# An encoder layer on one core: constant products and a pinned root at the start, stores on another queue, attention's pool in three, the last sums elsewhere

## The chip, the cores and the metric

The kernel runs on one core of one Trainium2 chip. A core has a matrix engine (TensorE; PE in the profile, with its weight loads as PEld), a vector engine (VectorE, DVE), an activation engine (ScalarE, ACT), a general engine (GpSimd, POOL) and a queue that mostly issues transfers (SyncE, SP). ACT issues transfers too; they stand in the profile as ACTq. Sixteen DMA engines move the data. Each engine works through its own instructions in the order in which they were laid down. The metric is the time of one execution in device microseconds; less is better.

## The reference, cut to what matters

One layer of a bidirectional encoder in float32, on 2048 rows of 1024 columns: a combined projection of the normed input, from which a Hyena part (long convolutions by FFT, 512 channels) and an mLSTM part (4 heads, both directions) are made; their output projection; cross-attention into 256 rows of `mem`; a squared-ReLU MLP; a final norm.

```python
u = _rms_norm(h, norm_mix_g[l])
proj = u @ w_in[l]
hy = _short_conv_centred(proj[..., :HY_COLS], hy_conv_w[l], hy_conv_b[l])
...
y_hy = _group_rms_norm(_hyena(hy, spec, hy_skip[l]), hy_norm_g[l], HYENA_GROUPS)
...
y_ml = _group_rms_norm(y_ml, ml_norm_g[l], MLSTM_HEADS)
mixed = jnp.concatenate([y_hy.astype(h.dtype), y_ml.astype(h.dtype)], axis=-1)
h = h + mixed @ w_out[l]
h = h + _cross_attention(_rms_norm(h, norm_x_g[l]), _rms_norm(mem, norm_mem_g[l]),
                         xa_wq[l], xa_wk[l], xa_wv[l], xa_wo[l])
h = h + jnp.square(jax.nn.relu(_rms_norm(h, norm_ff_g[l]) @ ff_w1[l])) @ ff_w2[l]
...
return _rms_norm(h, final_norm_g)
```

## The kernel before

**Products.** A float32 product is made of three products of rounded halves (`mm3`, L355): high by high, high by low, low by high, each 128x128 by 128x512, summed in a bank of PSUM. `split` (L367) makes the halves: ACT rounds, DVE subtracts. Two tags of four banks each, `mm` and `hy`, hold results.

**The order.** The code is a set of generators that hand over to each other (`program`, L2056): the input projection (`sweep`, `natural`) is woven with the filters, then with Hyena; the projections of `mem` (`memproj`, L684) with the first five steps of mLSTM (`take(m, 5)`, L2079); then attention (L1416) with the rest of mLSTM, by `weave`, which gives each side a share of time; then the MLP (`ffn`, L1772). What comes out is given to a planner, which orders each engine's instructions by its own estimate of times. An instruction that is *pinned* (`keep_in_program_order`) keeps its place among the pinned ones; `behind` puts an instruction after the last product so far.

**The start (L548).** The projection begins before the norm is known: the raw input, times the gain, is split into `xh` and `xl`, and the factor 1/rms of each row is applied when a bank is emptied (L780, by `rowb`). Of each half (c = 0, 1) of the first 1024 rows come: `operand` (the split), `squares` (ACT squares, DVE sums into `ssum`), `columns` (four products that sum over partitions, then `inv_rms` with a root by Newton steps in `rsqrt`, L224, then `diagonal`, which makes the tile `dg`), `rows` (a product that spreads the factors over partitions, copied to `rowb`). These pieces hang on hooks `(group, k)`: group is the number of the bank being filled, k the block of 128 inputs. Groups 0 to 3 are c = 0, 4 to 7 are c = 1, so the fifth group needs a bank that `rowb` has released.

**`memproj`.** For each of four heads `keys` multiplies a projection of `mem` with the query weights and stores four tiles `o` into `gd`; `values` does the same with the output weights into `vw`. A tile is copied out of its bank by ACT (`staged`, L704, tag `st`, three buffers) and stored from ACT's own queue (L718, L730). The weights of `mem` (`wm`) come over SP's queue. `natural` (L854) stores the mLSTM values and the sigmoid gates from ACT's queue too (L886).

**Pools.** `i_sb` (L437) holds all tiles of the projection phase. Attention's pool `t` (L1354) lies in the space that it and Hyena's pool leave, with `acc`, four activations, two pairs of weight halves and four staging tiles `wn`; what is first written there waits for the readers of what lay there. In attention `mixed` loads rows of Hyena's and mLSTM's outputs (L1452), turns them with the identity (L1458) and splits them; the first products of half the depth (L1510) need Hyena's rows alone.

**The end.** The second matrix of the MLP is done with seven products per pair of blocks (a Strassen-like scheme): seven sums `acc[i, tp]`, filled for four blocks o of the depth (L1965), and combined for the last block (o = 3) by `add` (L1958) on DVE (V) or POOL (G). `turned` turns a combined tile back, with its squares (L1929) and the gain (L1930); `finish` (L1932) takes the root and scales (L1942 on DVE, L1944 on ACT) and stores to the output. The last product of all is i = 4, tp = 1, and its four results are added at L1994.

Of the kernel before, what the change touches and what calls it, by code (L numbers as in the profile page):

```python
# [133 lines left out]
class Prog:  # L134
# [89 lines left out]
    def rsqrt(self, pool, ms, name):  # L224
# [5 lines left out]
        nc.vector.tensor_scalar(yi, mi, -0.5, float(0x5F3759DF), ALU.mult, ALU.add)  # L230
        for _ in range(3):
            nc.vector.tensor_tensor(t, y, y, ALU.mult)
            nc.vector.scalar_tensor_tensor(t, t, -0.5, ms, ALU.mult, ALU.mult)
            nc.vector.scalar_tensor_tensor(y, t, 1.5, y, ALU.add, ALU.mult)
# [147 lines left out]
    def weights(self, pool, w, n, kc=4, bufs=2, nbufs=2, pin=False):  # L382
# [4 lines left out]
        if n > 512:  # L387
            for k0 in range(kt):
                for c0 in range(0, n, 512):
                    cs = slice(c0, c0 + 512)  # L390
                    nat = pool.tile([128, 512], F32, tag="wn", name="wn", bufs=nbufs)
# [3 lines left out]
        for k0 in range(0, kt, kc):  # L395
            nat = pool.tile([128, kc, n], F32, tag="wn", name="wn", bufs=nbufs)
# [31 lines left out]
    def inproj_open(self, es):  # L428
# [7 lines left out]
        self.d_gt = self.dram("gt", (L, 16))  # L436
        sb = self.isb = es.enter_context(tc.tile_pool(name="i_sb", bufs=1))  # L437
# [21 lines left out]
    def inv_rms(self, dst, src):  # L459
        nc, sb, n = self.nc, self.isb, dst.shape[1]  # L460
        ms = sb.tile([128, 4], F32, tag="ms", name="ms", bufs=2)[:, 0:n]
        nc.vector.tensor_scalar(ms, src, 1.0 / D, EPS, ALU.mult, ALU.add)
        nc.vector.tensor_copy(dst, self.rsqrt(sb, ms, "xr"))

    def square_sum(self, x, dst):
        junk = self.isb.tile([128, 512], F32, tag="st", name="junk", bufs=3)
# [26 lines left out]
    def diagonal(self, cols):  # L493
        dg = self.isb.tile([128, 512], F32, tag="rb", name="dg", bufs=2)[:, 0:128 * cols.shape[1]]
        for t in range(cols.shape[1]):
            self.nc.vector.tensor_scalar(dg[:, 128 * t:128 * t + 128], self.ident, cols[:, t:t + 1], None, ALU.mult)
# [27 lines left out]
    def x_chunks(self, hf):  # L524
# [3 lines left out]
        def room(n):  # L528
            if not 1 < n < deep:
                return None  # L530
            t = self.isb.tile([128, 1088], F32, tag=("P", "cv")[n % 2], name="xt", bufs=2)
# [16 lines left out]
    def x_first(self):  # L548
# [10 lines left out]

        wsrc = self.items[0][0].rearrange("(k p) c -> p k c", p=128)  # L560
# [3 lines left out]
        for j in range(4):  # L564
            t = sb.tile([128, 1088], F32, tag=("P", "cv")[j // 2], name="xt", bufs=2)
# [5 lines left out]
        def operand(xs, c, k):  # L571
# [3 lines left out]
            nc.vector.scalar_tensor_tensor(self.xl[to], xs[k], g, self.xh[to].bitcast(F32), ALU.mult, ALU.subtract)  # L575

        def squares(xs, c):
            for k in range(8):
                sq = sb.tile([128, 512], F32, tag="st", name="sq", bufs=3) if k else ssum[c]
                pin(nc.scalar.activation(sq, xs[k], AF.Square))  # L580
                if k:
                    nc.vector.tensor_tensor(ssum[c], ssum[c], sq, ALU.add)

        def columns(c):
# [8 lines left out]
            self.inv_rms(rx, p[:, 0:4])  # L593
            self.dg = self.diagonal(rx)
# [1554 lines left out]
```

## Time and profile before

| | us |
|---|---|
| median of 3 runs | 3109.32 (3107.85 to 3111.45) |
| the profiled execution | 3110.14 |
| its span, first to last instruction | 3108.4 |
| PE busy | 3025.3 |
| DVE busy | 1955.3 |
| ACT busy | 1497.7 |
| POOL busy | 1141.1 |

A row of a timeline gives the start in us, the duration, engine, line, operation, what is written and read with the shapes, and in brackets the idle time before it and what released it. A row of waits gives the total, the number and the longest. A row of stretches gives the stretch and its length, the busy time of PE, PEld, DVE, ACT and POOL with counts, the granted TensorE clock (1 is full), the share of DMA time used, and GB/s. The clock has no record for the first 12 us; there the distance between products shows it.

### The profile page before, as it was taken

To read this page: it belongs to the slowest core of one execution; us is meant where nothing else is said; L and a number is where in the kernel's file an instruction comes from. 1 tells how busy PE (TensorE), PEld (TensorE's weight loads), DVE (VectorE), ACT (ScalarE), POOL (GpSimd) and SP (SyncE) were. 2 spreads that over 40 slices of the span, in tenths; PEclk is the share of its full clock that TensorE was granted. 3 is DMA by queue.
4 is the path that set the end of the run, shared out by engine and by line. 5 is a ranking of instruction groups with operands and counts; after the bars stand their busy time and mean duration, and the time that the engine had idled before them with its cause. 6 is when DMAs were issued, how large, how long until landed. Compare 5 with 4: busy or idle time off the path is not lost.

```text
span 3108.4 us, 42926 instructions
## 1 busy us (share of the span) xinstructions
PE 3025.3 (97%) x14257; PEld 2374.5 (76%) x14257; DVE 1955.3 (63%) x3429; ACT 1497.7 (48%) x2931; POOL 1141.1 (37%) x802
## 2 busy tenths in 40 slices
PE   8999999999999998999999999999999999999998
PEld 6655667776676766888887888888888788888876
DVE  7865465446756456877664566657554676565696
ACT  6543466533656225565544455556555443333335
POOL 0122011200222333333132337766466375243693
PEclk9999999999999999999999999999999999999999
DMA  6654768576878996565476557657644565354435
GB/s 211 190 198 163 231 207 251 178 232 194 254 203 241 302 300 220 158 199 170 143 250 206 197 172 235 207 178 238 200 153 153 171 210 182 109 166 118 157 93 172
DMA packets 444102, 607.07 MB, mean 195 GB/s; under 512 B 38494, under 2 KB 248542, under 8 KB 442856
## 3 DMA queue, kind: packets, MB, share of 16 engines
q1 hardware_dynamic: 405988, 546.54, 55.2%
q10 hardware_dynamic: 37892, 57.79, 5.5%
q8 instruction: 113, 1.85, 0.2%
q14 instruction: 109, 0.89, 0.1%
HBM read 401.79 MB, written 202.41 MB: 194 GB/s over the span
## 4 chain that ended last, share of the span: by engine, by line
PE 55%; DVE 3%; DMA 1%; issue 1%; ACT 1%; POOL 0%; SPq 0%; DVEq 0%; POOLq 0%; ACTq 0%
PE mm L361 12%; PE mm L357 12%; PE mm L360 12%; PE hy L357 6%; PE hy L361 6%; PE hy L360 6%; DVE bl L1668 1%; PE hy L1310 1%; PE hy L1312 1%; DVE acc L1960 0%; PE hy L1458 0%; DVE acc L1994 0%; PE hy L1571 0%; DMA va<-vd 0%; PE hy L1272 0%
## 5 line engine op out<-in xcount | busy, mean ns | idle before, releaser
L1668 DVE TENSOR_TENSOR bl<-wr,bh 128x512 fp32r<-128x512 f32 x213 | 242.1, 1142 | 127.6 <-ACT bh L1667 122.9
L1667 ACT CAST ah<-w 128x512 fp32r<-128x512 f32 x284 | 176.5, 622 | 301.1 <-PE hy L360 155.9
L368 DVE TENSOR_TENSOR wl<-wn,wh 128x512 fp32r<-128x512 f32 (+1 forms) x296 | 213.1, 765 | 101.0 <-ACT wh L368 100.4
L357 PE MATMUL mm<-xh,wh 128*128 128x512 f32 x640 | 267.5, 419 | 8.5 <-ACT wh L368 7.9
L1024 POOL TENSOR_TENSOR b<-b,a 128x512 f32<-128x512 f32 x64 | 87.0, 1362 | 509.4 <-ACT b L1022 238.8
L360 PE MATMUL mm<-xl,wh 128*128 128x512 f32 x640 | 253.7, 397 | 1.3 <-DVE xl L368 1.3
L361 PE MATMUL mm<-xh,wl 128*128 128x512 f32 x640 | 254.8, 399 | 0.0
L1667 ACT CAST bh<-wr 128x512 fp32r<-128x512 f32 x232 | 143.5, 621 | 230.2 <-PE mm L361 172.6
L1668 DVE TENSOR_TENSOR al<-w,ah 128x512 fp32r<-128x512 f32 x236 | 216.0, 916 | 55.5 <-ACT ah L1667 54.1
L357 PE MATMUL mm<-bh,ah 128*128 128x512 f32 x576 | 225.2, 391 | 1.8 <-DVE acc L1830 1.7
L361 PE MATMUL mm<-bh,al 128*128 128x512 f32 x576 | 223.3, 390 | 2.6 <-POOL al L1668 2.6
L360 PE MATMUL mm<-bl,ah 128*128 128x512 f32 x576 | 224.4, 390 | 0.0
L368 ACT CAST wh<-wn 128x512 fp32r<-128x512 f32 (+1 forms) x296 | 164.2, 618 | 109.4 <-PE mm L361 52.7
L360 PE MATMUL mm<-act,wh 128*128 128x512 f32 x512 | 202.3, 395 | 0.0
L361 PE MATMUL mm<-act,wl 128*128 128x512 f32 x512 | 200.5, 393 | 0.9 <-DVE wl L368 0.9
L357 PE MATMUL mm<-act,wh 128*128 128x512 f32 x512 | 199.6, 396 | 1.3 <-ACT wh L368 1.2
L357 PE MATMUL hy<-bh,ah 128*128 128x512 f32 x448 | 175.2, 391 | 0.0
L360 PE MATMUL hy<-bl,ah 128*128 128x512 f32 x448 | 174.6, 390 | 0.0
L361 PE MATMUL hy<-bh,al 128*128 128x512 f32 x448 | 174.4, 390 | 0.0
L357 PEld LDWEIGHTS mm<-xh,wh 128*128 128x128 f32 x640 | 121.1, 189 | 60.8 <-issue 18.6
L357 PE MATMUL mm<-wh,xh 128*128 128x256 f32 (+1 forms) x512 | 156.0, 305 | 3.8 <-ACT xh L368 2.3
L361 PEld LDWEIGHTS mm<-xh,wl 128*128 128x128 f32 x640 | 121.0, 189 | 47.8 <-issue 23.2
(375 smaller groups left out, 8225.4 us busy)
## 6 DMA issues: line engine op xcount, KB each, us to landing
wr<-hc SPq DMA_DIRECT2D x224, 256.0 KB
w<-in_ff_w_dram SPq DMA_DIRECT2D x172, 256.0 KB
hc<-wn SPq DMA_DIRECT2D x128, 256.0 KB
wn<-in_w_in_dram SPq DMA_DIRECT2D x100, 256.0 KB
hc<-q SPq DMA_DIRECT2D x96, 256.0 KB
fs<-a SPq DMA_DIRECT2D x32, 512.0 KB
a<-fs SPq DMA_DIRECT2D x64, 256.0 KB
a<-zs SPq DMA_DIRECT2D x64, 256.0 KB
```

Source lines behind the costliest of these rows:

```text
L357: first = mm(ps, lh, rh, start=start, stop=False)
L360: mm(ps, lh, rl, start=False, stop=False)
L361: self.last = mm(ps, ll, rh, start=False, stop=stop)
L368: both = (self.nc.scalar.copy(hi, src), self.nc.vector.tensor_tensor(lo, src, hi.bitcast(F32), ALU.subtract))
L1024: nc.gpsimd.tensor_tensor(xt, xt, hi[:, m], ALU.mult)
L1310: nc.tensor.matmul(dst, nm[:, h], va[:, h], start=True, stop=state is None)
L1312: nc.tensor.matmul(dst, rows_[d, 1][:, h], state[:, h], start=False, stop=True)
L1667: self.nc.scalar.copy(hi, src)
L1668: eng.tensor_tensor(lo, src, hi.bitcast(F32), ALU.subtract)
```

## The change

Seven edits, in the order of the program. (1) Fifteen 128x128 products of constants ahead of the first loads; the steps of the first half's root and its diagonal are pinned, as are the later operands and sums of the second half; the hooks are moved, and every first product of a k in groups 2 and 3 is pinned. (2) Tiles `cv` and `wn` get a pool `i_w` of their own, tiles `st` a pool `i_st`. (3) Stores of the keys, and of the gates of one column block (c2 = 2), go from ACT's queue to SP's; keys alternate between staging tiles of both pools. (4) Attention's pool becomes `t_w` (one pair of weights), `t_acc`, `t` (two activations, the other pair) and `t_n` (the rest). (5) Four steps of mLSTM instead of five go beside `memproj`, and two steps each of attention and mLSTM are taken in turn before the weave. (6) Among the last sums: acc 5 is added to acc 3 before the last block, by POOL, and the last block's product is added to both; acc 6 to acc 3 by DVE instead of POOL; acc 7 to acc 4 later; one weight block is split by DVE. (7) The scalings that fall into the last product are laid behind its last sums and go to POOL instead of DVE; in the last row block one tile more goes to DVE.

```diff
+    def rsqrt(self, pool, ms, name, keep=lambda ins: ins):
...
+        keep(nc.vector.tensor_scalar(yi, mi, -0.5, float(0x5F3759DF), ALU.mult, ALU.add))
         for _ in range(3):
+            keep(nc.vector.tensor_tensor(t, y, y, ALU.mult))
...
+        sw = self.isw = es.enter_context(tc.tile_pool(name="i_w", bufs=1))
+        for tag, n, bufs in (("cv", 1088, 2), ("wn", 544, 4)):
+            for _ in range(bufs):
+                sw.tile([128, n], F32, tag=tag, name=tag, bufs=bufs)
+        self.ist = es.enter_context(tc.tile_pool(name="i_st", bufs=1))
...
+        p = self.hy()
+        for _ in range(15):
+            nc.tensor.matmul(p[:, 0:128], self.ones, self.ones, start=True, stop=True)
...
+            if c and k > 1:
+                pin(d)
...
+            keep = (lambda ins: ins) if c else pin
+            self.inv_rms(rx, p[:, 0:4], keep)
+            self.dg = self.diagonal(rx, keep)
...
-        self.hooks = {(0, 5): second, (1, 5): lambda: operands(range(4)), (2, 5): lambda: columns(0), (2, 6): halfway,
-                      (3, 5): lambda: rows(0), (5, 1): lambda: columns(1), (5, 6): lambda: rows(1), (6, 0): third}
+        self.hooks = {(0, 5): second, (1, 5): lambda: operands(range(2)), (2, 4): lambda: columns(0),
+                      (2, 5): lambda: operands(range(2, 8)), (3, 1): lambda: rows(0), (3, 3): lambda: squares(x1, 1),
+                      (5, 5): lambda: columns(1), (6, 0): third, (6, 2): lambda: rows(1)}
...
+        def staged(p, wide=False):
+            if wide:
+                o = self.isw.tile([128, 2, 256], F32, tag="wn", name="o", bufs=4)
+            else:
+                o = self.ist.tile([128, 2, 256], F32, tag="st", name="o", bufs=3)
...
-                nc.scalar.dma_start(out=gd[h // 2, :, 2 * i2:2 * i2 + 2, cs], in_=staged(p))
+                nc.sync.dma_start(out=gd[h // 2, :, 2 * i2:2 * i2 + 2, cs], in_=staged(p, i2 % 2 == 0))
...
-                                 k == 0 and 3 < self.made < 13 or hook and self.made in (2, 3))
+                                 k == 0 and 3 < self.made < 13 or self.made in (2, 3))
...
+                (nc.sync if c2 == 2 else nc.scalar).dma_start(
+                    out=(self.d_vd if c2 < 2 else self.d_od)[r0:r0 + 128, 256 * (c2 % 2):256 * (c2 % 2) + 256], in_=so)
...
-        T = self.T = es.enter_context(self.tc.tile_pool(name="t", bufs=1))
-        self.acc = T.tile([128, 8, 512], F32, name="acc")
+        self.wp = [pool("t_w"), None]
+        for tag in ("wh", "wl"):
+            self.wp[0].tile([128, 8, 256], F32R, tag=tag, name=tag)
+        self.acc = pool("t_acc").tile([128, 8, 512], F32, name="acc")
+        self.wp[1] = self.ap = pool("t")
...
+        self.T = pool("t_n")
+        self.acts = self.wps = 0
...
+        return (self.ap if (self.acts - 1) // 2 % 2 else self.T).tile([128, 8, 512], F32R, tag="act", name=name, bufs=2)
...
-            eng = nc.vector if n < 6 else nc.gpsimd
+            eng = nc.vector if n < 6 or n == 25 else nc.gpsimd
...
+                if scalings is None:
+                    scale(c, dst, rv)
+                else:
+                    scalings.append(lambda: scale(c, dst, rv, nc.gpsimd))
...
-                        if h and c % 2 == 0:
-                            nc.vector.tensor_scalar(v, v, rv[:, t:t + 1], None, ALU.mult)
+                        if h and c % 2 == 0 or last and t == 3:
+                            eng.tensor_scalar(v, v, rv[:, t:t + 1], None, ALU.mult)
...
+                if s + 4 == len(down):
+                    scalings = []
...
+                        if o == 3 and i == 5:
+                            w = acc[3, tp][:, m]
+                            nc.vector.tensor_tensor(w, bank[m], w, ALU.add)
...
+                for f in scalings or ():
+                    f()
+                scalings = None
+                if o == 2 and i == 5:
+                    add(3, 5, tp, G)
...
-                    add(3, 6, tp, G)
+                    add(3, 6, tp, V)
                 elif i == 5:
-                    add(3, 5, tp, V)
                     add(5, 7, tp, G)
-                    add(4, 7, tp, G)
...
                 elif i == 3:
+                    if tp:
+                        add(4, 7, 0, G)
...
                 elif i == 2:
+                    if not tp:
+                        add(4, 7, 1, G)
...
-                             p.turned_in(), take(n, 2), beside_each(n, take(m, 5)))
+                             p.turned_in(), take(n, 2), beside_each(n, take(m, 4)))
...
                 g = p.attention(at)
+                for x in (g, m, g, m):
+                    next(x)
                 weave(g, m, 440, 112, True)
```

More of the change, by code (lines that the diff above doesn't have):

```diff
@@ L620, in operands @@
                 operand(x1, 1, k)
-        def halfway():
-            operands(range(4, 8))
-            squares(x1, 1)
         def third():
```

83 lines of the change are left out of this document (38 added, 45 removed).

## The prediction, made before the changed kernel was run

> **What bounds the kernel now.** I read the page first, then the waits of TensorE (PE), then busy time by stretches, and then the order of time in the stretches where PE is not full.
>
> ```profile
> span 3108.4 us, 42926 instructions
> PE 3025.3 (97%) x14257; PEld 2374.5 (76%) x14257; DVE 1955.3 (63%) x3429; ACT 1497.7 (48%) x2931; POOL 1141.1 (37%) x802
> ```
>
> PE is busy for 97% of the span. No edit removes a matmul that counts, so all that can be won is PE's idle time, 3108.4 - 3025.3 = 83 us, and what its matmuls lose at a reduced clock. The waits name the places (total us, times, longest):
>
> ```profile
> PE mm L357 <- ACT wh L368: 9.2, 2, 7.9
> PE hy L1188 <- ACT ht L1324: 7.6, 1, 7.6
> PE hy L598 <- DVE dg L496: 4.7, 1, 4.7
> PE hy L1458 <- DMA wn<-yh: 4.4, 1, 4.4
> PE hy L1458 <- DVE act L368: 4.3, 1, 4.3
> PE mm L716 <- ACT o L706: 3.4, 2, 3.1
> PE mm L716 <- ACT kt L701: 2.4, 1, 2.4
> PE mm L699 <- ACT o L706: 2.0, 1, 2.0
> ```
>
> The 7.9 us are the first loads and stay. The stretches around the others (columns: PE, PEld, DVE, ACT, POOL busy, granted clock, DMA share, GB/s):
>
> ```profile
> 20.00:40.00 20.00, 15.32 (x61) 11.64 (x61) 15.73 (x38) 10.74 (x18) 0.00 (x0) 0.83 0.42 148
> 60.00:80.00 20.00, 20.00 (x90) 15.98 (x90) 18.90 (x45) 13.99 (x28) 0.00 (x0) 1.00 0.71 224
> 1060.00:1080.00 20.00, 15.62 (x55) 11.39 (x56) 6.74 (x21) 2.84 (x6) 4.38 (x3) 0.83 1.04 339
> 1100.00:1120.00 20.00, 16.93 (x64) 12.65 (x63) 8.09 (x20) 2.45 (x5) 8.65 (x6) 0.83 1.06 325
> 1180.00:1200.00 20.00, 11.35 (x72) 8.89 (x72) 15.44 (x42) 11.84 (x45) 11.42 (x9) 0.93 0.73 228
> 1200.00:1220.00 20.00, 14.77 (x72) 13.55 (x73) 13.91 (x45) 9.78 (x34) 3.90 (x4) 0.73 0.82 285
> 3000.00:3010.00 10.00, 8.34 (x37) 6.57 (x35) 10.00 (x11) 1.36 (x3) 9.37 (x7) 1.00 0.35 105
> 3010.00:3020.00 10.00, 7.78 (x36) 6.10 (x37) 10.00 (x10) 5.04 (x11) 10.00 (x7) 1.00 0.46 141
> ```
>
> Four places, then: the start, the projections of mem with a saturated DMA (share above 1), the passage to attention around 1200 us, and the last sums around 3000 us, where DVE and POOL are both full. A clock of 0.83 over 20 us is 6.8 us at half speed ((1 - 0.83) / 0.5 x 20), so a wait is paid again when PE resumes. To these comes the tail behind the last matmul.
>
> **The change part by part.** *Start.* The order of time:
>
> ```profile
> 0.93 0.17 DVE L150 MEMSET ones<- 128x128 f32 x1
> 8.95 0.63 PE L357 MATMUL mm<-xh,wh 128*128 128x512 f32 x1
> 9.38 0.63 PE L360 MATMUL mm<-xl,wh 128*128 128x512 f32 x1
> 20.06 0.39 PE L360 MATMUL mm<-xl,wh 128*128 128x512 f32 x1
> 20.29 0.39 PE L361 MATMUL mm<-xh,wl 128*128 128x512 f32 x1
> 22.20 0.69 DVE L582 TENSOR_TENSOR ssum<-ssum,sq 128x512 f32<-128x512 f32 x1
> 28.00 0.95 PE L587 MATMUL hy<-ones,ssum 128*128 128x1 f32 x8
> 29.67 0.17 DVE L230 TENSOR_SCALAR xr_y<-ms 128x4 int32<-128x4 int32 x1
> 33.65 0.16 DVE L233 SCALAR_TENSOR_TENSOR xr_t<-xr_t,ms 128x4 f32<-128x4 f32 x1
> 33.84 0.16 DVE L234 SCALAR_TENSOR_TENSOR xr_y<-xr_t,xr_y 128x4 f32<-128x4 f32 x1
> 34.90 0.88 DVE L496 TENSOR_SCALAR dg<-ident,small 128x128 f32<-128x128 f32 x4
> 35.83 2.07 PE L598 MATMUL hy<-dg,ones 128*128 128x512 f32 x2 [4.68 <-DVE dg L496]
> ```
>
> Products start 0.43 us apart at 9 us and 0.23 us at 20 us: the first ten or so run at half clock and lose 10 x 0.2 = 2.0 us. The fifteen constant products come ahead of them. The nearest row is L598, a cold 128x512 product in 2.07 us, so a 128-column one takes a quarter, 0.52 us or less; fifteen from 1.1 us (ones written) end at 8.9 us if all are cold, near 7 us if the clock comes after 4.5 us as it did for the products. The first real product waits for its weights until 7.93 us: free, or at worst 1 us late and warm. *The root:* between 29.67 and 34.90 us lie ten steps of 0.2 us pitch, stretched by sums of squares put between them. Pinned, they take 12 x 0.2 + 0.88 = 3.3 us, and the fifteen products that the new hooks leave between columns and rows take 15 x 0.227 = 3.4 us. So the 4.7 us wait for dg goes, and what the half-speed matmuls behind it lose: 6.8 us cold, of them 2.1 to 5.2 at work, half of that lost, and I take 2.1. What is late next: columns moves from about the 79th product (10 cold + (28.0 - 12.3) / 0.227) to the 60th, which PE, warm, reaches at 7.93 + 60 x 0.227 = 21.5 us. The sum of squares ends at 22.9 us, so PE waits 1.4 us. The second set of squares, pinned, can also stand before the multiply that frees the first bank, up to 7 x 0.6 = 4 us of it; I count 2.4. The second root is only later: fifteen products stand between its two hooks as before, and no wait on it is in the list; 0, or 4.7 again if they don't cover it. Gain 2.0 + 4.7 + 2.1 - 1.4 - 2.4 = 5.0, between 1 and 8.8.
>
> *Keys and gates.* 16 stores of keys and 16 of gates go from ACT's queue to SP's. ACT shows why that matters: it finishes a copy at 1095.2 us and gets its store issued only at 1104.8 us.
>
> ```profile
> 1094.58 0.59 ACT L706 COPY o<-mm 128x512 f32<-128x512 f32 x1
> 1104.78 0.37 ACTq L718 DMA_DIRECT2D gd<-o  x1
> ```
>
> For 9.6 us nothing else on ACT runs, and PE waits for a bank. The wait rows of L716 and L699 sum to 7.8 us; the clock of 0.83 in two stretches is 13.6 us at half speed, at most 6.8 lost: 14.6 at most. Wider staging (four tiles more, alternating) helps likewise. But the DMA is full there, and the bytes stay, except those of the one mLSTM step that take(m, 4) puts later: six loads of 256 KB, 1.57 MB, at the 339 GB/s of the row 4.6 us. The gates' stores lie in calmer stretches and bring 0. I take 4.6, between 0 and 14.6. The Trainium skill ("DMA: Bandwidth & Descriptors", section "Issuing engines are not separate DMA queues") says that transfers from any issuer run on the same 16 DMA engines and that spreading the issue saves issue time alone. By it this term is what the bytes allow; the blocked issue on ACT is a wait that the sentence does not speak of, and the trace shows it.
>
> *Attention's pool made of three.*
>
> ```profile
> SPq L1452 <- DMA vw<-o: 5.0, 2, 2.5
> 1192.17 2.18 ACT L368 CAST wh<-we 128x512 fp32r<-128x512 f32 x4 [0.30 <-DMA vw<-o]
> 1213.35 1.57 PE L357 MATMUL mm<-act,wh 128*128 128x512 f32 x4
> ```
>
> Attention's first row loads (L1452) and its first weights, loaded long before, both wait for the last store of the values: the new pool lies over the old one. The first half products (48 x 0.227 = 10.9 us) so begin at 1213 us, while PE idles 8.65 + 5.23 = 13.9 us in 1180 to 1220 and has 13.6 us of half clock, at the busy share there (26.1 of 40) 8.9 us of work, 4.4 lost. With weights over a pool that the keys leave, and rows over space that Hyena leaves, those 10.9 us can fill the gap and keep the clock: at most 10.9 + 4.4 = 15.3. The second pair of weights still waits for the last product of the values, and one mLSTM step more stands here, a chain of some 10 us that would add 4 with nothing beside it. I take 9.0, between -4 and 15.3.
>
> *Last sums.*
>
> ```profile
> L1960 POOL TENSOR_TENSOR acc<-acc 128x512 f32<-128x512 f32 x32 | 50.9, 1610 | 15.6 <-DVE acc L1960 10.2 <-DVE acc L1994 5.4
> 3007.76 3.43 DVE L1960 TENSOR_TENSOR acc<-acc 128x512 f32<-128x512 f32 x2
> 3062.06 1.16 DVE L234 SCALAR_TENSOR_TENSOR or_y<-or_t,or_y 128x4 f32<-128x4 f32 x1
> 3091.25 2.48 DVE L1994 TENSOR_TENSOR acc<-hy,acc 128x512 f32<-128x512 f32 x4
> ```
>
> Of POOL's 32 adds 16 leave the crowded stretch (8 go to DVE, 8 to calmer times), 8 come from DVE earlier, and eight operations of one weight block go to DVE. DVE gets 16 operations more there (8 from PSUM at 0.62, 8 at 0.62 to 1.7), 10 to 19 us, but an add takes it 0.62 us from PSUM with POOL idle (3091 us) and 1.7 us between SBUF tiles beside a full POOL (3007 us). PE's idle time here is 1.66 + 2.22 = 3.9 us. I take 2.0, between -3 and 3.9. *Tail:* four scalings (1.6 us) no longer stand before the last four adds at 3091.25 us; they go to POOL. 1.6 at most, nothing if DVE's roots are held up by POOL as in the row at 3062 us (1.16 against 0.16 us). I take 1.2. The Trainium skill ("SBUF — State Buffer", section "SBUF: two separate sides") calls the port pair that VectorE and GpSimd share an exclusive lock, held for the whole instruction; by it the move of scalings to GpSimd may cost DVE one such operation, and the two rows agree.
>
> The weave starts anew behind four hand-made steps, so mLSTM runs ahead of attention by some 10 us of PE work. The wait L1458 <- wn (4.4 us) may go or another come: 0, within 6 either way. A planner orders everything by its own clock; that has no row.
>
> **Sum.** 5.0 + 4.6 + 9.0 + 2.0 + 1.2 = 21.8 us off the profiled execution's 3110.1 us (span 3108.4) is 3088.3; the median of the runs is 0.8 lower, so 3087.5 us. The terms' half widths (4, 7, 9, 3, 1, 6), as independent, give about 14, an own range of 3074 to 3102.
>
> **The rivals.**
> (a) *Everything is had:* 8.8 + 14.6 + 15.3 + 3.9 + 1.6 = 44.2, 3065.1 us. For it: PE waits for ACT alone, never for a load, in the saturated stage. Against: DMA share above 1. 0.08.
> (b) *The passage stays and the DMA is the bound.* The planner keeps attention's first products behind the values, and the projections run at the DMA's pace: 5.0 + 2.0 + 1.2 = 8.2, 3101 us. For it: 16 DMA engines full; the Trainium skill's sentence above leads here. Against: the named release is one store. 0.17.
> (c) *The start too is swallowed:* DVE is busy 18.9 of 20 us at 60 to 80 us, and what arrives earlier may queue there; 3.2 are left, 3106 us. Against: DVE itself idles 4.3 us of 20 to 40 us, which it gets back. 0.07.
> (d) *Slower: SP stands still instead of ACT.* The blocked issue moves to the queue that does nearly all loads.
>
> ```profile
> SPq L822 <- ACT st L206: 62.3, 24, 5.4
> ```
>
> SP already waits 2.6 us per such store. Blocks of 9.6 us at two or three stores, some 21 us in which no load is issued, become PE's wait from the point where a block outlasts the lead of the loads behind it; less today's 7.8 that is 13, with two restarts at half clock 4 more, and the passage, whose loads are on that queue, gains nothing: +17 against 8.2 gained, 3118 us. Against: the weights of mem are issued tens of us ahead. 0.10.
>
> **How the numbers follow.** The forecast has 0.58. From about 0.2% (6 us) on, a measurement of this kernel can tell a difference. Faster: 0.57 + 0.08 + 0.13 of (b) = 0.78. Slower: 0.10 + 0.01 = 0.11. The rest, 0.11, is within. The range 3068 to 3108 leaves out (d), most of (a) and a part of (c), under 2 in 10.
>
> **What would show it.** Right: no wait of L598 on dg above 1 us, products 0.23 us apart from the first on, no ACT gap ahead of a store of keys, wh of attention written before 1190 us, under 6 us of idle in the 40 us around the passage, DVE below 10 of 10 around 3000 us, the last adds starting right at the last product. Wrong: new waits of PE on loads between 1040 and 1200 us, SP waiting for a copy while loads stand behind it, or waits on DVE between 40 and 100 us.

## The result, and the profile after

| | before | changed |
|---|---|---|
| median, us | 3110.27 (8 runs) | 3121.07 (8 runs, 3116.04 to 3123.38) |
| ratio, 95% interval | | 1.0032 [1.0021, 1.0043] |

The change makes the kernel 10.8 us slower; 21.8 us faster was forecast, and the time lies outside the range.

The page of the changed kernel, first lines. PE is busy for 5.5 us more (the constant products alone take 5.9), and the span grew by 11.0 us: PE's idle time went from 83.1 to 88.6 us.

```profile
span 3119.4 us, 43012 instructions
PE 3030.8 (97%) x14287; PEld 2381.0 (76%) x14287; DVE 1953.9 (63%) x3442; ACT 1496.2 (48%) x2930; POOL 1131.9 (36%) x798
```

The start of the changed kernel, in order of time on PE:

```profile
1.13 5.89 PE L567 MATMUL hy<-ones 128*128 128x128 f32 x30 [1.13 <-DVE ones L150]
7.94 0.50 PE L357 MATMUL mm<-xh,wh 128*128 128x512 f32 x1 [0.92 <-ACT wh L368]
...
8.51 0.40 PE L357 MATMUL mm<-xh,wh 128*128 128x512 f32 x1
8.74 0.39 PE L360 MATMUL mm<-xl,wh 128*128 128x512 f32 x1
...
23.01 1.05 PE L599 MATMUL hy<-ones,ssum 128*128 128x1 f32 x8 [1.16 <-DVE ssum L592]
27.91 1.13 PE L611 MATMUL hy<-dg,ones 128*128 128x512 f32 x2 [0.30 <-DVE dg L501]
```

This is what was forecast: the constants end at 7.0 us, the real products start at 7.94 us and stand 0.23 us apart from the third on, the sum of squares costs 1.16 us and `dg` 0.30 in place of 4.68. The Trainium skill ("TensorE: Matmul & The Clock Gate", the part on the clock gate) gives about 3.4 us of sustained work until the clock is full; the trace agrees, since 5.9 us of constants were enough.

The stretches of the changed kernel that answer to those of before (columns as there), and behind them two of before:

```profile
20.00:40.00 20.00, 18.54 (x82) 14.15 (x81) 18.09 (x42) 12.62 (x21) 0.00 (x0) 1.00 0.42 147
1060.00:1080.00 20.00, 17.05 (x75) 13.02 (x76) 7.98 (x19) 3.49 (x8) 6.27 (x4) 1.00 1.06 350
1100.00:1120.00 20.00, 19.52 (x86) 13.45 (x87) 7.92 (x21) 1.95 (x4) 9.34 (x7) 1.00 1.05 339
1120.00:1140.00 20.00, 14.35 (x54) 9.31 (x53) 4.77 (x17) 7.39 (x28) 3.75 (x3) 0.83 1.06 348
1160.00:1180.00 20.00, 14.69 (x81) 11.18 (x80) 8.16 (x26) 8.79 (x27) 9.12 (x7) 0.92 0.83 266
1180.00:1200.00 20.00, 10.39 (x54) 8.87 (x54) 14.32 (x49) 9.76 (x36) 6.30 (x5) 0.66 0.74 254
1200.00:1220.00 20.00, 20.00 (x117) 17.84 (x116) 14.08 (x45) 9.85 (x41) 6.79 (x5) 0.91 0.42 132
3000.00:3010.00 10.00, 10.00 (x46) 8.28 (x45) 10.00 (x12) 2.50 (x4) 6.92 (x5) 1.00 0.20 65
3010.00:3020.00 10.00, 9.61 (x43) 7.62 (x41) 8.60 (x12) 1.77 (x3) 4.82 (x5) 1.00 0.26 79
3020.00:3030.00 10.00, 6.29 (x23) 5.13 (x24) 9.16 (x15) 3.92 (x8) 4.77 (x5) 0.83 0.54 161
```

```profile
1120.00:1140.00 20.00, 18.16 (x86) 11.78 (x86) 11.01 (x37) 8.90 (x31) 9.41 (x7) 1.00 1.01 345
1160.00:1180.00 20.00, 19.80 (x96) 13.45 (x94) 10.15 (x44) 10.69 (x37) 6.23 (x5) 1.00 0.71 229
```

The holes at 1060 and 1100 us are smaller, as forecast, but the one at 1120 has grown to 5.65 us (1.84 before), and one of 5.31 us opens at 1160 us, where PE had been busy for 19.8 of 20. The hole of the passage is earlier, not gone: 1160 to 1220 us lacks 14.9 us, where it lacked 14.1 before. In the last sums the hole is still there, with a piece at reduced clock: it stands at 3020 us, which is the place of 3008 us before, since this kernel runs 12 us late by then.

The waits of PE in the changed kernel (total, times, longest) name the new holes; four of those shown are steps of mLSTM (L1198, L1320).

```profile
PE hy L1198 <- ACT ht L1334: 8.3, 2, 5.6
...
PE hy L1320 <- DVE ht L1354: 4.7, 3, 2.8
PE hy L1320 <- DVE hy L220: 4.2, 1, 4.2
PE mm L361 <- DVE al L1687: 4.1, 1, 4.1
PE hy L1320 <- ACT rw L1291: 4.0, 1, 4.0
```

And ACT's wait ahead of a store did not vanish. In the changed kernel it is a store of the *values* that waits, and for longer, 12.1 us from the end of the copy to the issue (9.6 before). The changed kernel, then the row of before behind its own wait:

```profile
1111.88 0.56 ACT L719 COPY o<-mm 128x512 f32<-128x512 f32 x1
1124.56 0.38 ACTq L743 DMA_DIRECT2D vw<-o  x1
1125.04 0.58 ACT L719 COPY o<-mm 128x512 f32<-128x512 f32 x1 [12.59 <-DMA a<-zg]
```

```profile
1105.24 0.59 ACT L706 COPY o<-mm 128x512 f32<-128x512 f32 x1 [10.07 <-DMA wm<-in_xa_wo_dram]
```

In both kernels the profile ends ACT's idle time with the landing of a transfer (`wm`, `a`). So this looks like a wait for another transfer, and not like the time of the issue itself; why the store has to wait for it is not shown.

A view of the whole is the *lag*: the start of the same product in a kernel's trace less its start in the trace of before, for a few products of PE. Each column is a single execution, and executions of one kernel lie up to 14 us apart here (before: 3103.77 to 3117.40), so a lag is good to a few us; the verdicts rest on all executions. The columns other than the first are experiments of the next section.

```
before, us  product                 changed  ends   wide   pools  queue  share+ share-
                                             e1     e10    e14    e15    e16    e13
1017        Hyena, last but one     -6.4     -4.2   -5.8   -6.5   -1.2   -5.8   -3.1
1184        values, last            -15.2    -1.6   -15.5  -10.3  -9.0   -7.3   -16.6
1193        mLSTM L1312, a quarter  +14.2    -1.5   +6.8   -10.3  -9.1   -7.9   +13.5
1520        attention           +5.2   -1.5   +0.4  -10.2   -9.3   -9.2   -2.8
1564        attention, half         +13.8    -1.3   +0.5   -9.9   -9.1   -0.6   -2.8
2990        MLP, nine tenths        +11.8    -3.5   -2.3   -11.4  -11.6  -2.0   -4.5
3093        last turn               +10.9    -4.7   -3.3   -13.2  -13.2  -2.0   -6.3
```

In the changed kernel the projections of mem run 15 us ahead, while mLSTM's steps beside them fall 14 us behind. Attention's products are 5.2 us late at 1520 us and 13.8 at 1564 us, so another 8.6 us are lost between these two; from there nothing more is lost.

### The profile page after: what moved, and what is told of

The parts are those of the page before. It is cut to its first block, busy times and chain, and to the rows that moved or that the text cites. A ratio compares the mean times of both kernels' runs of the same rounds, so it can differ in the third digit from the quotient of the medians.

```text
span 3119.4 us, 43012 instructions
## 1 busy us (share of the span) xinstructions
PE 3030.8 (97%) x14287; PEld 2381.0 (76%) x14287; DVE 1953.9 (63%) x3442; ACT 1496.2 (48%) x2930; POOL 1131.9 (36%) x798
## 4 chain that ended last, share of the span: by engine, by line
PE 78%; DMA 9%; DVE 6%; ACT 2%; issue 2%; POOL 1%; SPq 1%; ACTq 0%; DVEq 0%; POOLq 0%
PE mm L357 16%; PE mm L361 16%; PE mm L360 16%; PE hy L361 6%; PE hy L357 6%; PE hy L360 6%; PE hy L178 3%; PE mm L956 2%; PE hy L987 1%; PE hy L1029 1%; DMA a<-hy 1%; DMA a<-zg 1%; PE hy L1198 1%; DMA yh<-a 1%; PE hy L1320 1%
## 5 line engine op out<-in xcount | busy, mean ns | idle before, releaser
L368 DVE TENSOR_TENSOR wl<-wn,wh 128x512 fp32r<-128x512 f32 (+1 forms) x296 | 223.0, 797 | 113.3 <-ACT wh L368 112.5
L361 PEld LDWEIGHTS mm<-xh,wl 128*128 128x128 f32 x640 | 120.1, 188 | 46.2 <-issue 21.8
```

The costliest lines, as they stand in the source:

```text
L361: self.last = mm(ps, ll, rh, start=False, stop=stop)
L368: both = (self.nc.scalar.copy(hi, src), self.nc.vector.tensor_tensor(lo, src, hi.bitcast(F32), ALU.subtract))
```

## The experiments

Each kernel is the one before or the changed one with some of the edits. Differences from before are those of the medians, from executions of both on the same chip; the ratio is worked out from all executions and can differ a little (e14_pools_no_wide: 10.2 us by the medians, 7.8 by the ratio). The intervals are 0.09 to 0.17% either way, 3 to 5 us, so a difference of 3 us between two kernels cannot be told for certain.

| run | what it is | median, us | before, us | ratio [95%] |
|---|---|---|---|---|
| e1_ends | start, last sums, last scalings | 3100.49 | 3109.70 | 0.9971 [0.9961, 0.9982] |
| e2_stores_act | changed, stores back on ACT | 3124.05 | 3109.70 | 1.0043 [1.0026, 1.0060] |
| e3_order_back | changed, order of before | 3106.81 | 3109.70 | 0.9992 [0.9982, 1.0001] |
| e4_one_pool | changed, one pool for attention | 3114.99 | 3109.70 | 1.0018 [1.0009, 1.0028] |
| e5_pools_alone | ends + three pools | 3098.40 | 3110.32 | 0.9958 [0.9943, 0.9973] |
| e6_stores_alone | ends + staging + stores | 3105.47 | 3110.32 | 0.9985 [0.9975, 0.9994] |
| e7_order_alone | ends + new order | 3112.77 | 3110.32 | 1.0005 [0.9995, 1.0016] |
| e8_four_steps | changed, no steps in turn | 3114.12 | 3110.32 | 1.0017 [1.0007, 1.0027] |
| e9_start_tail | start, last scalings | 3100.49 | 3110.45 | 0.9968 [0.9957, 0.9979] |
| e10_wide_alone | ends + pools i_w, i_st + wider staging | 3105.83 | 3110.45 | 0.9986 [0.9976, 0.9995] |
| e11_open_later | changed, MLP laid down later | 3120.73 | 3110.45 | 1.0032 [1.0021, 1.0043] |
| e12_start_tail_pools | start, scalings, three pools | 3101.11 | 3110.45 | 0.9969 [0.9956, 0.9981] |
| e13_share_less | changed, mLSTM's share 104 | 3104.70 | 3108.94 | 0.9988 [0.9979, 0.9997] |
| e14_pools_no_wide | ends + pools i_w, i_st | 3098.75 | 3108.94 | 0.9975 [0.9964, 0.9987] |
| e15_queue_alone | ends + stores on SP | 3097.55 | 3108.94 | 0.9960 [0.9947, 0.9973] |
| e16_share_more | ends, mLSTM's share 116 | 3107.74 | 3108.94 | 0.9999 [0.9990, 1.0009] |
| e17_no_wide_old_order | changed, old staging, old order | 3098.94 | 3112.39 | 0.9957 [0.9942, 0.9971] |
| e18_no_wide_share | changed, old staging, share 104 | 3096.60 | 3112.39 | 0.9957 [0.9943, 0.9971] |

### First: which part loses

Theory 1 was that the projections run ahead and mLSTM loses its cover, theory 2 that the new order is to blame, theory 3 the pools. **e1_ends** takes edits 1, 6 and 7 of the change alone, among them:

```diff
+        for _ in range(15):
+            nc.tensor.matmul(p[:, 0:128], self.ones, self.ones, start=True, stop=True)
...
-                    add(3, 6, tp, G)
+                    add(3, 6, tp, V)
...
+                    scalings.append(lambda: scale(c, dst, rv, nc.gpsimd))
```

> The kernel before with the start, the last sums and the last scalings of the change, and nothing of the middle. If the start's 4.9 us and the tail's 1.7 us, read from the trace of the changed kernel, stand by themselves and the last sums bring about -0.7, the median is 5 to 7 us under before: 3103 to 3105. If what the start wins is swallowed later also without the middle edits (rival c), it is 3108 to 3111.

Measured 9.2 us under before, more than the 5 to 7 expected: the ends stand by themselves, and rival (c) is out.

**e2_stores_act** undoes the queue in the changed kernel (the line of the keys; the gates go back as well):

```diff
-                nc.sync.dma_start(out=gd[h // 2, :, 2 * i2:2 * i2 + 2, cs], in_=staged(p, i2 % 2 == 0))
+                nc.scalar.dma_start(out=gd[h // 2, :, 2 * i2:2 * i2 + 2, cs], in_=staged(p, i2 % 2 == 0))
```

> The changed kernel with the stores of keys and gates back on ACT's queue. Theory 1 (the keys' stores on SP let the projections of mem run ahead of the chain of mLSTM, which so loses its cover at 1160 to 1200 us): the projections no longer lead by 15 us, the half clock near 1177 us shortens, and the median falls to 3102 to 3108. Theory 2 (the order: four steps of mLSTM beside the projections and steps taken in turn ahead of the weave): nothing comes back, 3117 to 3123. Theory 3 (the pool made of three): the same, 3117 to 3123.

3124.05 us, not less than the changed kernel: the stores on SP are not what loses. Theory 1 as put is wrong about the queue.

**e3_order_back** undoes the order:

```diff
-                             p.turned_in(), take(n, 2), beside_each(n, take(m, 4)))
+                             p.turned_in(), take(n, 2), beside_each(n, take(m, 5)))
...
-                for x in (g, m, g, m):
-                    next(x)
```

> The changed kernel with the order of before: five steps of mLSTM beside the projections of mem, and the weave starting at once. Theory 2 (the order costs the 17 us): 3099 to 3105, with the transfers near 1550 us no longer late. Theory 1: the projections still run ahead and the cover is still gone: 3115 to 3122. Theory 3: 3117 to 3123.

2.9 us under before and 13.7 us better than the change, 2 us above the range of theory 2: the order is the largest loss. But with the ends' 9.2 us in it, it still lacks 6 us to them.

**e4_one_pool** gives attention its single pool back:

```diff
-        self.wp = [pool("t_w"), None]
...
-        self.T = pool("t_n")
+        T = self.T = es.enter_context(self.tc.tile_pool(name="t", bufs=1))
```

> The changed kernel with attention's pool in one piece again; the stores, the wider staging and the order stay. Theory 3 (the three pools move the loads of attention and of the MLP so that they collide): 3100 to 3106. Theories 1 and 2: the pool release is worth little, 3117 to 3126, since attention's weights and rows came early in the changed kernel and PE did not use it.

5.3 us over before. This is 5.5 us better than the change, between the theories: beside the other edits the three pools cost something.

### Second: each middle part on the ends alone

**e5_pools_alone** adds edit 4 (the diff of e4_one_pool, the other way round), **e6_stores_alone** edits 2 and 3, **e7_order_alone** edit 5 (the diff of e3_order_back, the other way round). **e8_four_steps** takes only the loop over (g, m, g, m) out of the changed kernel. The line of e6_stores_alone that matters:

```diff
-                nc.scalar.dma_start(out=gd[h // 2, :, 2 * i2:2 * i2 + 2, cs], in_=staged(p))
+                nc.sync.dma_start(out=gd[h // 2, :, 2 * i2:2 * i2 + 2, cs], in_=staged(p, i2 % 2 == 0))
```

> The start, last sums and last scalings of the change plus attention's pool made of three; staging, stores and order of before. If the release of the pool is what the prediction took it for, 9.0 us come off the 3100.5 us of the ends alone: 3091 to 3094. If the passage is bound by the chain of the mLSTM steps that stand ahead of attention's products in PE's order, the early rows and weights are worth nothing: 3099 to 3103. If the pools themselves cost what came back when they were undone in the changed kernel (6 us): 3105 to 3108.

11.9 us under before, 2.7 better than the ends, near the second of the three cases. The timelines of e5_pools_alone (SP, then ACT, then PE) show why so little:

```profile
1160.11 1.56 SPq L1463 DMA_DIRECT2D wn<-yh  x3
```

```profile
1184.23 2.16 ACT L368 CAST wh<-we 128x512 fp32r<-128x512 f32 x4
```

```profile
1193.38 2.09 PE L1190 MATMUL hy<-ve,kn 128*128 128x129 f32 x8 [7.58 <-ACT ht L1326]
1195.26 2.77 PE L1469 MATMUL hy<-ident,wn 128*128 128x128 f32 x12
...
1204.54 1.32 PE L357 MATMUL mm<-act,wh 128*128 128x512 f32 x4
```

The pool did what it says: attention's rows are loaded from 1160.11 us on (1192.09 before) and its weights are written at 1184.23 (1192.17). PE starts its transposes at 1195.26 us all the same, directly behind a step of mLSTM that waits 7.58 us for ACT, because that step stands ahead of them in PE's order. The wait of 7.6 us was in the list of before, to the tenth.

> The start, last sums and last scalings plus the wider staging and the stores of keys and gates on SP; one pool, order of before. As predicted (4.6 us off): 3095 to 3098. If the projections of mem only run ahead and are then missing as cover for the mLSTM steps: the projections lead by about 10 us, the step near 1193 us is late by some 10 us, and the median is 3103 to 3108.

4.8 us under before, so 4.4 of the ends' 9.2 us are lost again, as the second case had it.

> The start, last sums and last scalings plus four steps of mLSTM beside the projections and the steps taken in turn; stores, staging and pool of before. If the order alone costs what came back when it was undone (14 us): 3112 to 3117, with half the cost near 1200 us and half near 1550 us. If the order costs only where the projections run ahead: 3100 to 3105.

2.4 us over before: 11.6 us lost to the ends without any other edit.

> The changed kernel without the two steps each taken in turn ahead of the weave; four steps of mLSTM beside the projections stay. If the fifth step, moved behind the projections, is what is paid: as the changed kernel, 3117 to 3123, with the passage late by 9 us or more. If the steps taken in turn shift the weave so that transfers meet near 1550 us: 8 us less, 3110 to 3114.

3.8 us over before, 7 less than the change, at the edge of the second case. The steps taken in turn are about half of the order's cost; what the fourth step pays is not settled by this run.

### Third: inside the parts

**e9_start_tail** is e1_ends with the last sums of before (`add(3, 6, tp, G)` and the other lines of edit 6):

> The start and the last scalings alone, with the last sums of before. If the last sums are worth nothing, as the traces of the changed kernels have it (their lag does not fall between 2990 and 3085 us): as the ends together (3100.5 us), 3099 to 3102. If they are worth the 2.0 us of the prediction: 3102 to 3104.

10.0 us under before without the last sums, 9.2 with them: they are worth nothing that can be told.

**e10_wide_alone** has the separate pools and the wider staging, and the old queue.

> The start, last sums and last scalings plus the wider staging alone; all stores on ACT's queue as before. If the wider staging is what lets the projections run ahead (with the keys' stores back on ACT they still led by 10 us): projections ahead by 8 us or more and 3103 to 3107. If it takes the stores on SP: projections at most 4 us ahead, 3099 to 3102.

4.6 us under before, 4.6 us of the ends lost, as the first case. New pools and wider staging come together here; e14_pools_no_wide below takes them apart.

**e11_open_later** was to delay the MLP's loads in the changed kernel:

```diff
+                for _ in range(2):
+                    next(g)
                 ms.close()
                 p.ffn_open(rs)
```

> The changed kernel with two steps of attention laid down between the end of mLSTM and the opening of the MLP, so that the MLP's first loads stand where they stood before, behind 37 steps of attention and not behind 35. If it is these loads that meet attention's own near 1550 us: about 8 us back, 3111 to 3115, and PE full between 1530 and 1570 us. If the loss there has another cause (the mLSTM rows themselves, a wait of DVE): 3118 to 3124.

Nothing came back, but nothing had moved either: on SP's queue the MLP's loads (`wr<-in_ff_w`, `w<-in_ff_w`) still stand in the midst of attention's `wn<-vw` (issued at 1532.69, then the MLP's at 1534.39, then `wn<-vw` again at 1549.91 us). The planner, not the order of the text, placed them, and mLSTM still ended behind 35 steps of attention. The run says nothing about the cause.

**e12_start_tail_pools** is e9_start_tail with edit 4.

> The start, the last scalings and attention's pool made of three, all else as before. If the ends bring 9 us and the pools 2, as they did with the last sums added: 3097 to 3100, faster than both kernels. If the pools' 2 us were chance: 3100 to 3102.

9.3 us under before, no better than the start and the tail alone: with e5_pools_alone, the three pools are worth between nothing and 3 us.

### Fourth: the two causes by themselves

**e14_pools_no_wide** differs from e10_wide_alone in one argument; **e16_share_more** differs from e1_ends in one number, and **e13_share_less** from the changed kernel in the same one, 104 for 112:

```diff
-                nc.scalar.dma_start(out=gd[h // 2, :, 2 * i2:2 * i2 + 2, cs], in_=staged(p, i2 % 2 == 0))
+                nc.scalar.dma_start(out=gd[h // 2, :, 2 * i2:2 * i2 + 2, cs], in_=staged(p))
```

```diff
-                weave(g, m, 440, 112, True)
+                weave(g, m, 440, 116, True)
```

> The ends plus the separate pools for cv, wn and st, with the keys' tiles all in the old staging. If the lead of the projections is what costs the passage its cover: the projections lead by 4 us at most, the step near 1193 us is not late, and the median is 3099 to 3102. If the separate pools themselves cost it: 3104 to 3107 as with the wider staging.

10.2 us under before: without the second staging the loss is gone, so giving half of the keys' tiles to it costs 5.6 us by the medians. The two intervals overlap; the last part of this section has the same pair twice more, with intervals that do not. PE's order in e10_wide_alone around the last projections (L741 values, L1282 and L1320 mLSTM):

```profile
1151.62 10.46 PE L741 MATMUL mm<-wm,kt 128*128 128x512 f32 x24
1161.92 1.05 PE L1282 MATMUL hy<-qn,kk_t 128*128 128x128 f32 x8
...
1172.30 1.16 PE L1282 MATMUL hy<-qn,kk_t 128*128 128x128 f32 x8 [1.42 <-DVE cf L1204]
...
1184.66 0.77 PE L1320 MATMUL hy<-va,rw 128*128 128x129 f32 x2 [9.42 <-DVE bry L218]
```

and in e14_pools_no_wide:

```profile
1148.48 1.05 PE L1282 MATMUL hy<-qn,kk_t 128*128 128x128 f32 x8
...
1155.97 1.88 PE L741 MATMUL mm<-wm,kt 128*128 128x512 f32 x4
...
1158.58 8.75 PE L741 MATMUL mm<-wm,kt 128*128 128x512 f32 x20
1167.17 1.05 PE L1282 MATMUL hy<-qn,kk_t 128*128 128x128 f32 x8
```

With the old staging, projections and steps of mLSTM alternate. With the wider one a run of 24 products stands ahead of the step at 1161.92 us, and the last eight follow within it. The next step, at 1172.30 us, has nothing beside it: PE waits 9.42 us in one piece. On ACT of e10_wide_alone this wait goes back to

```profile
1176.61 1.28 ACT L1192 ACTIVATE ve<-va,cols 128x129 f32<-128x129 f32 x4 [3.31 <-DMA va<-vd]
```

which waits 3.31 us for a load of mLSTM and has the rest of the chain behind it in ACT's order. From 1160 to 1220 us PE lacks 19.9 us in e10_wide_alone and 12.9 in e14_pools_no_wide; from 1040 to 1160 us, where the projections stand, it lacks 7.3 and 9.3.

**e15_queue_alone** moves the stores of keys and gates to SP on top of e1_ends, and nothing else of the middle:

```diff
-                nc.scalar.dma_start(out=gd[h // 2, :, 2 * i2:2 * i2 + 2, cs], in_=staged(p))
+                nc.sync.dma_start(out=gd[h // 2, :, 2 * i2:2 * i2 + 2, cs], in_=staged(p))
```

> The ends plus the stores of keys and gates on SP, with the staging of before. As predicted for the stores: up to 4.6 us off the ends' 3100.5, 3096 to 3099. If freeing ACT's queue only makes the projections run ahead: 3103 to 3107 with the step near 1193 us late. If the stores on SP change nothing, because the staging tiles and not the queue hold the projections: 3099 to 3102.

11.4 us under before, 2.2 better than the ends: in direction the first case, but less than can be told for certain. What ACT waits for in e15_queue_alone has changed its name:

```profile
1095.45 1.26 ACT L711 COPY o<-mm 128x512 f32<-128x512 f32 x2 [8.64 <-DMA gd<-o]
```

Now it is the tile that is late: its old content has not landed yet. The Trainium skill ("DMA: Bandwidth & Descriptors", section "Issuing engines are not separate DMA queues") has it that another issuer saves the time of the issue only; the trace agrees here, 8.64 us of waiting beside 9.6 before.

> The changed kernel with a smaller share for mLSTM in the weave (104 for 112), so that mLSTM ends, and the MLP is opened, behind 37 steps of attention as before, and not behind 35. If the earlier opening is what costs 8 us near 1550 us: 3111 to 3115, PE full between 1530 and 1570 us. If not: 3118 to 3124.

4.2 us under before: 15.0 us come back from one number, twice what was expected.

> The kernel with the ends alone and a larger share for mLSTM in the weave (116 for 112), so that the MLP is opened behind 35 steps of attention and not behind 37; nothing else differs. If the earlier opening costs 8 us near 1550 us: 3107 to 3111. If the opening has no price: 3099 to 3102.

1.2 us under before: the same number, moved the other way, takes 8.0 of the ends' 9.2 us. SP's order in e16_share_more:

```profile
1521.39 0.88 SPq L1385 DMA_DIRECT2D wn<-vw  x2
...
1523.07 1.39 SPq L1760 DMA_DIRECT2D wr<-in_ff_w_dram  x2
1524.54 5.71 SPq L1717 DMA_DIRECT2D w<-in_ff_w_dram  x4
...
1539.63 0.41 SPq L1385 DMA_DIRECT2D wn<-vw  x1
```

and in the kernel before:

```profile
1524.87 16.26 SPq L1383 DMA_DIRECT2D wn<-vw  x8
...
1561.40 0.98 SPq L1758 DMA_DIRECT2D wr<-in_ff_w_dram  x2
```

Before, attention's eight loads of `vw` are out before the MLP's first weights are asked for. In e16_share_more the MLP's weights stand in their midst. The consequence there on ACT and PE:

```profile
1549.70 0.63 ACT L1498 ACTIVATE sq<-acc 128x512 f32<-128x512 f32 x1 [4.91 <-DMA wn<-vw]
```

```profile
1550.89 0.55 PE L357 MATMUL mm<-act,wh 128*128 128x512 f32 x1 [2.59 <-ACT wh L368]
```

The stretches of e16_share_more (DMA share 0.96 and 0.91 in the last two) and, below, of e13_share_less:

```profile
1500.00:1520.00 20.00, 16.41 (x95) 13.79 (x93) 13.29 (x46) 9.25 (x31) 1.29 (x1) 1.00 0.43 133
1520.00:1540.00 20.00, 18.57 (x85) 15.42 (x86) 13.97 (x19) 12.39 (x23) 8.22 (x6) 0.91 0.96 296
1540.00:1560.00 20.00, 17.41 (x70) 13.82 (x69) 10.79 (x10) 7.35 (x13) 14.15 (x10) 0.91 0.91 326
```

```profile
1500.00:1520.00 20.00, 20.00 (x110) 17.11 (x109) 12.40 (x33) 11.97 (x36) 1.23 (x1) 1.00 0.22 69
1520.00:1540.00 20.00, 19.95 (x114) 16.61 (x113) 12.29 (x26) 12.70 (x34) 3.08 (x2) 1.00 0.42 138
1540.00:1560.00 20.00, 20.00 (x90) 16.55 (x89) 12.88 (x33) 9.78 (x18) 6.99 (x5) 1.00 1.00 348
```

PE lacks 7.6 us in the first, 0.05 in the second. Not all of the 7.6 us can be the MLP's loads: 3.6 of them stand in 1500 to 1520 us, ahead of the first MLP weights at 1523.07 us. There PE waits for mLSTM's last rows, which attention loads and turns as soon as they are stored (waits of e16_share_more from 1495 to 1560 us):

```profile
PE hy L1460 <- DMA wn<-ym: 2.4, 2, 1.7
PE hy L1460 <- DVE act L368: 1.4, 1, 1.4
```

So an earlier end of mLSTM has two prices here: its last rows are needed at once, and the MLP's loads stand among attention's, with 4.0 us of waits and a clock of 0.91. When it ends can be counted in the program: `weave` opens the MLP when mLSTM has ended. Before, attention has then made 37 steps. The four steps in turn of the change shift the shares, and it has made 35 (two in turn, 33 in the weave). The share of 104 makes it 37 again, that of 116 makes it 35 in the ends' kernel. In the six kernels in which mLSTM ends behind 35 steps (the changed one, e2_stores_act, e4_one_pool, e7_order_alone, e11_open_later, e16_share_more) the lag grows by 7.4 to 9.5 us between attention's products at 1520 and at 1564 us; in those in which it ends behind 37 it changes by less than half a us. e8_four_steps, which has 41, lets all eight loads of `vw` out together again.

That accounts for some 8.6 of the 15.0 us of e13_share_less. About 7 more lie between 1250 and 1520 us, where the lag goes from +1.0 to +5.2 us in the changed kernel and from +0.3 to -2.8 in e13_share_less; what costs them is not shown.

### Fifth: without the two causes

**e17_no_wide_old_order** and **e18_no_wide_share** are the changed kernel with `staged(p)` for the keys, the first with the old order (the diff of e3_order_back), the second with the new order and the share of 104:

```diff
-                nc.sync.dma_start(out=gd[h // 2, :, 2 * i2:2 * i2 + 2, cs], in_=staged(p, i2 % 2 == 0))
+                nc.sync.dma_start(out=gd[h // 2, :, 2 * i2:2 * i2 + 2, cs], in_=staged(p))
...
-                weave(g, m, 440, 112, True)
+                weave(g, m, 440, 104, True)
```

> The changed kernel with the keys' tiles in the old staging and the order of before; start, stores on SP, separate pools, attention's pool of three, last sums and last scalings stay. If the two causes are the whole loss and the gains add: 12 us under before for ends and stores, less 1 to 2 for the pools, some 13 us in all, 3095 to 3098 at a before of 3109 to 3110. If the freed queue and the pools let the projections run ahead also without the wider staging: 3100 to 3105.

> The changed kernel with the keys' tiles in the old staging and the share of 104 in the weave; all seven edits but for these two numbers. If the order itself is neutral once the MLP opens where it did: the 3104.7 us of the smaller share less the 5 to 7 us of the staging, 3097 to 3100. If four steps of mLSTM beside the projections cost the passage: 3101 to 3106.

Both are at a ratio of 0.9957, some 13 us under before (9 to 18 by the intervals; 13.5 and 15.8 by the medians), and with e15_queue_alone (0.9960) and e5_pools_alone (0.9958) the fastest of all. For e17_no_wide_old_order that is the size that its first case named. e18_no_wide_share shows that the new order is neutral once the MLP opens where it did. e17_no_wide_old_order differs from e3_order_back, and e18_no_wide_share from e13_share_less, by the argument of `staged` alone. These two pairs, whose intervals do not overlap, put the price of the wider staging beside the other edits at 10.6 and 11.6 us, about twice the 5.6 us on the ends alone. What made the change slow is one argument, and a share in the weave that was not fitted to the new order.

## Why the prediction was wrong, by its own steps

**Start: right.** The terms of the first 60 us, 2.0 + 4.7 + 2.1 - 1.4, make 7.4, and the lag of the changed kernel at 60 us is -7.3 us; with the 2.4 us that were to be given back 5.0 was forecast, and the lag from 150 to 1000 us is about -5 us. That it fits so closely is in part luck: in single executions of the 19 kernels that have this start, the lag at 200 us lies between -2.6 and -6.1 us. And the 10.0 us of start and tail by the medians (e9_start_tail) are 3 more than the traces show for the two; where these come from is open.

**Last sums: mis-sized; tail: right.** 2.0 was forecast for the sums and nothing can be told (e9_start_tail against e1_ends). POOL was relieved (46.8 us busy from 2970 to 3050 us, 66.9 before), DVE hardly (70.7, 71.3). The wait for `al`, 2.4 us on POOL before, became one of 4.1 us on DVE: it is the weight block whose split the change gave to DVE, where it stands behind eight additions. The tail brought 1.6 us by the lag (12.5 us at 3077, 10.9 at 3093), 1.2 were forecast. All ends together: 8.2 forecast, 9.2 measured.

**Keys and gates: the queue right in direction, the staging wrong.** The term of 4.6 us held two edits. The queue alone brought about 2.2 (e15_queue_alone), which the intervals cannot tell from nothing. The sentence "Wider staging ... helps likewise" is the failed step: it cost 5.6 us on the ends alone (e10_wide_alone against e14_pools_no_wide) and 10.6 to 11.6 beside the other edits. The prediction treated every wait of the projections on ACT as a loss. Where the projections cover a serial chain, their end sets nothing; running them 5 us further ahead (lags of -15.5 against -10.3 us in that pair) only leaves that chain alone.

**Attention's pool: the mechanism was there and released nothing on the path.** 9.0 was forecast, 0 to 3 us came (e5_pools_alone, e12_start_tail_pools). The failed step is "those 10.9 us can fill the gap". It named the releaser of the weights and the rows, the store of the values, and did not ask what stood ahead of their reader on PE. The row that would have told it, PE's 7.6 us for `ht`, stood in its list of waits. Rival (b) came near this: "The planner keeps attention's first products behind the values"; it is mLSTM that they are kept behind, and not the values.

**The weave: this is the largest error.** "0, within 6 either way" was the term; it cost 15.0 us (e13_share_less against the changed kernel), 11.6 on the ends alone. The prediction saw that mLSTM would run ahead and asked what waits for attention, not what begins when mLSTM ends.

Put together from the differences: -10.0 for start and tail, +0.8 last sums, +5.6 staging, -2.2 queue, about -1 pools, +15.0 weave give +8.2 us; measured +10.8. Taken from the other side, e18_no_wide_share is 15.8 us under before, the wider staging adds 11.6 (e13_share_less) and the share 15.0 (the changed kernel), which makes +10.8. So beside the other edits the staging costs more than by itself, and the pools, worth about 1 us alone, cost 5.5 (e4_one_pool). Why these prices rise together is not explained.

**The rivals.** (d) gave 3118 us and came near by its number, not by its cause: with the stores on SP alone the kernel is not slower than the ends (e15_queue_alone), and no hole of PE was traced to a load that a store of keys held back on SP. What was missing was a rival in which the new order itself loses.

## What to carry to other kernels

Ahead of a wait that an edit removes, look for what stands before the waiting instruction on its own engine: if that is a chain that waits for itself, the earlier operand buys nothing. Work that is dense and early is also cover; before letting it run ahead, name the chain that it covers. And where generators share time by weights, count at which step of the one the other ends, before and after the edit, for what opens there brings its own transfers.

## What the runs showed of the hardware

With the DMA share above 1, ACT stood still for 9.6 us ahead of a store, and in the changed kernel for 12.1, until a transfer landed; when the stores of the keys moved to SP, ACT was found waiting for the staging tile, 8.64 us. The chains of mLSTM keep PE at work but not at its clock: in 1160 to 1200 us of the changed kernel PE is busy for 25.1 of 40 us and has 16.8 us at half clock by the granted 0.92 and 0.66. The Trainium skill ("TensorE: Matmul & The Clock Gate", the part on the clock gate) names an idle window of about 3.4 us as what lowers the clock; single waits of 4.0 and 4.2 us stand here, but the low clock lasts four times as long as either. In stretches of 2 us the clock is 0.50 from 1178 to 1192 us, though PE is busy for 7.1 of these 14 us.
